# Weights of a hybrid decoder step split by transfers instead of by two engines

## The chip, the cores and the metric

The kernel runs on one core of one Trainium2 chip. Its time is the device time of one execution in microseconds, the median of three runs. The core has five engines with a queue of instructions each: TensorE (PE, its weight loads shown as PEld), VectorE (DVE), ScalarE (ACT), GpSimd (POOL) and SyncE (SP). Each runs its own queue in order; a waiting instruction holds up everything behind it on that queue. Transfers between memory (DRAM) and the core's buffers are issued from one of these queues and carried out by 16 DMA engines that all queues share.

## What is computed

One inference step of a two-layer decoder, for a prompt of 512 tokens and for 8 sequences of 8 new tokens, with the same weights; here all 576 tokens (NT) go through the dense products together. Cut to what matters:

```python
# layer A: gated linear attention (GLA), 4 heads
q, k, v, r, glow = split(rmsnorm(h, g_norm_a) @ w_in_a)        # 2048 x 6160
logg = log_sigmoid(glow @ w_gate_up + b_gate) / 16
o, S = gla_chunked(q, k, v, logg, s0)
h = h + (rmsnorm(o, g_onorm_a) * silu(r)) @ w_out_a            # 2048 x 2048
# shared keys and values, layer B: attention over a window of 128 with sinks, 32 heads
k, v = split(rmsnorm(h, g_norm_kv) @ w_kv)                     # 2048 x 512
q, z = split(rmsnorm(h, g_norm_b) @ w_in_b)                    # 2048 x 4096
h = h + (sink_attention(q, k, v) * silu(z)) @ w_out_b          # 2048 x 2048
y = rmsnorm(h, g_final)
```

Everything is float32. TensorE multiplies a rounded 32-bit format here (`float32r`), so each operand is split: its high part is the value rounded to that format, its low part is the rest. A product is taken as high x high, high part of the weights x low part of the input, and low part of the weights x high part of the input.

## The kernel before

The weights lie in DRAM as blocks of 128 output columns, each 128 partitions x 2048 numbers (16 k-tiles of 128 x 128). There are 48 blocks in `wA`, 16 in `wOA`, 4 in `wKV`, 32 in `wB` and 16 in `wOB`. `dense` makes the product of one block with all tokens. It loads the block in two halves of 8 k-tiles (512 KB each) with `load_w` (L171 to L174), a transfer issued from SP into one of three `raw` buffers. Each half is split in two quarters by `split_w` (L167 to L169): ScalarE casts a quarter of `raw` to the high part `wh`, VectorE subtracts that from `raw` into the low part `wl`; four buffers of a quarter each exist of both. Then `dense_mm` (L176 to L182) issues for every k-tile six products of 128 x 128 weights with 288 tokens: `wh` with the input's high and low part, `wl` with the input's high part, each for two halves of the tokens. They are summed in PSUM (`pd`), and a function `evac` takes the sum over.

The input's parts are the 16 tiles `X[k]`, split once per stage by ScalarE and VectorE (L96 and L97, L101 and L102).

The stages follow one another: the first two blocks and the low-rank gate while the input comes in; the 46 other blocks of `wA`, with the gated linear attention of the four heads running beside them as background chains (`gla_fronts`, `gla_backs`, `gla_samples`); the output projection `out_a` (16 blocks, with POOL adding up squares at L119 and SP storing `dh1`); four blocks for keys and values; the 32 blocks of `wB` with attention (`unit`, `unit_sample`) beside them; and the last projection, 13 blocks through `dense` and 3 that are loaded and split ahead into tiles `w` of their own and computed by halves of the tokens.

Nobody writes the order of the instructions out by hand. The program text interleaves the chains, and then a scheduler in the tile framework lays out each engine's queue from a model of how long things take and of when buffers come free. In attention, POOL's queue holds small copies into the score tiles `s` (L848 and L910; three such tiles exist).

Of the kernel before, what the change touches and what calls it, by code (L numbers as in the profile page):

```python
# [28 lines left out]
def f32(ap):  # L29
    return ap.bitcast(F32)  # L30
# [7 lines left out]
def kernel(ctx: ExitStack, tc: tile.TileContext, A, O):  # L38
# [82 lines left out]
    def make_rstd(src, n, out, b, lo=0, hi=NT):  # L121
        """out[:, t] = (sum over partitions of src[:, t] / n + eps) ** -0.5, on every partition,
        exp(-ln / 2) refined by a step of Newton's; in steps, with the banks of b"""
# [17 lines left out]
    def rstd_soon(srcs, n, b, lo, hi):  # L141
        """the same for the sum of srcs, left in the first bank of b; by columns, for few tokens"""
# [22 lines left out]
    WB = 4  # L165
# [5 lines left out]
    def load_w(wdram, blk, hf):  # L171
        raw = wp.tile([128, 8, 128], F32, tag="raw", name=nm("raw"), bufs=3)
        dma(raw, wdram[blk, :, hf * 1024:(hf + 1) * 1024].rearrange("p (k n) -> p k n", n=128))
        return raw  # L174
# [9 lines left out]
    def dense(wdram, blk, evac):  # L184
        p = pd.tile([128, 2, 512], F32, tag="d", name=nm("pd"))
        raws = [load_w(wdram, blk, hf) for hf in range(2)]
        for qt in range(4):
            wh = wp.tile([128, 4, 128], F32R, tag="wh", name=nm("wh"), bufs=WB)
            wl = wp.tile([128, 4, 128], F32R, tag="wl", name=nm("wl"), bufs=WB)
            split_w(raws[qt // 2][:, (qt % 2) * 4:(qt % 2) * 4 + 4, :], wh, wl)  # L190
            for kk in range(4):
                dense_mm(p, qt * 4 + kk, wh[:, kk, :], wl[:, kk, :], (0, 1))
                if kk % 2 == 1:
                    yield
        evac(p[:, :, :HT])
# [3 lines left out]
    def run(fg):  # L199
        """trace fg, with the steps of the background chains between its own"""  # L200
# [24 lines left out]
    with tc.tile_pool(name="gp", bufs=1) as gp:  # L225
        # ================= layer A ========================================
# [37 lines left out]
        # low-rank gate: the columns [wh | wl] three times, so that the rows of its  # L264
        # output carry what the stacked operand of the next product needs
# [9 lines left out]
        # the first two blocks and the gate's product, together as x comes in  # L275
# [12 lines left out]
        for k in range(KT):  # L288
            if k % 4 == 0:
                w0 = []  # L290
                for blk in range(2):
                    w0.append([wp.tile([128, 4, 128], F32R, tag=t, name=nm(t), bufs=WB) for t in ("wh", "wl")])
                    split_w(raws0[blk, k // 4], *w0[blk])
            split_gain(k, hpt(k), GA)
            (sso if k % 3 == 1 or k > 11 else sse).add(hpt(k))
            for blk in range(2):
                dense_mm(held[blk], k, w0[blk][0][:, k % 4, :], w0[blk][1][:, k % 4, :], (0, 1))
# [74 lines left out]
        def chunk_front(h, c, p, r):  # L372
            """scores (transposed, into scT), scaled q and k of a chunk, or of the samples (whose
            keys come twice); p is the chunk's PSUM bank"""
# [104 lines left out]
            # the pairs with their diagonal, and k by token  # L479
# [89 lines left out]
        def gla_samples():  # L569
            for h in range(NH):  # L570
# [13 lines left out]
                # for each half of the sequences: every product of a high or low part of k  # L584
                # with a high or low part of v has its rows
# [592 lines left out]
```

## Time and profile before

| | |
|---|---|
| median of 3 runs | 1793.08 us (1791.33 to 1793.31) |
| profiled execution, first to last instruction | 1791.2 us |
| PE busy | 1767.2 us (99%) |
| DVE busy | 1117.0 us (62%) |
| ACT busy | 780.5 us (44%) |
| POOL busy | 110.1 us (6%) |
| moved by the DMA engines | 231.02 MB, 129 GB/s in the mean |
| mean granted TensorE clock | 0.996 |

The profiled execution's own time is that span; the page gives no other for it. An engine's busy share does not say what bounds it. Matmuls overlap in the record, so a busy PE is judged by the pace of its instructions and by what it waited for. In the rows below a line such as `L168 ACT CAST wh<-raw 128x512 fp32r<-128x512 f32 x452 | 279.4, 618 | 589.8 <-PE pd L180 577.5` reads: the instructions of code line 168 on ScalarE, writing wh from raw, 452 of them, 279.4 us in all and 618 ns each; before them the engine stood idle for 589.8 us, 577.5 of which ended when TensorE was done with something of line 180.

### The profile page before, as it was taken

Reading aid. Unit: us, or ns where it says so; the run is one execution under the profiler, and the core shown is the slowest. Engines: PE = TensorE matmul, PEld = TensorE weight load, DVE = VectorE, ACT = ScalarE, POOL = GpSimd, SP = SyncE. Lnnn points to the kernel's source line nnn. Section 1 sums busy time; section 2 is a strip of 40 time slices with the busy share of each in tenths; the row PEclk is TensorE's granted clock in tenths of the full one; section 3 lists DMA queues with packets and bytes.
Section 4 is the critical chain, followed back from the end, with each engine's and each line's share of the span. In section 5 each row is a group of like instructions: output and inputs, shape, how many; then the busy total and the mean of one; then the engine's idle time right before and its main releaser. Section 6 shows DMA issues by size and latency. Waiting matters only on the chain.

```text
span 1791.2 us, 33731 instructions
## 1 busy us (share of the span) xinstructions
PE 1767.2 (99%) x13152; PEld 1748.8 (98%) x13152; DVE 1117.0 (62%) x2539; ACT 780.5 (44%) x1632; POOL 110.1 (6%) x190
## 2 busy tenths in 40 slices
PE   8999999999999999999999999999999999999997
PEld 7999999999999999999999999999999999999996
DVE  8576776786776886544222566888888873442234
ACT  7533334334444344343222555667666652332231
POOL 3000001001001001000010100100000000001110
PEclk9999999999999999999999999999999999999998
DMA  8245643564564343223333444343332222223323
GB/s 301 89 160 176 195 156 117 176 197 136 161 194 158 119 154 135 96 77 124 128 131 127 134 134 110 88 126 101 105 99 88 85 94 82 83 98 108 104 106 106
DMA packets 118767, 231.02 MB, mean 129 GB/s; under 512 B 22064, under 2 KB 49584, under 8 KB 118576
## 3 DMA queue, kind: packets, MB, share of 16 engines
q1 hardware_dynamic: 118608, 228.88, 39.4%
q8 instruction: 103, 1.69, 0.4%
q14 instruction: 56, 0.46, 0.1%
HBM read 174.57 MB, written 43.65 MB: 122 GB/s over the span
## 4 chain that ended last, share of the span: by engine, by line
PE 94%; issue 2%; DMA 2%; DVE 1%; ACT 0%; POOL 0%; POOLq 0%; DVEq 0%; SPq 0%; ACTq 0%
PE pd L180 79%; PE pb L463 2%; PE pb L863 1%; PE pb L550 1%; DMA hp<-in_xT_dram 1%; PE pb L846 1%; PE pb L639 1%; PE pb L638 1%; PE pb L636 1%; PE pb L845 1%; PE pb L551 1%; PE pb L873 1%; PE pb L874 1%; PE pb L481 1%; PE pb L558 0%
## 5 line engine op out<-in xcount | busy, mean ns | idle before, releaser
L180 PE MATMUL pd<-x,wh 128*128 128x288 f32 x7232 | 1305.0, 298 | 9.8 <-ACT x L96 6.7
L180 PEld LDWEIGHTS pd<-x,wh 128*128 128x128 f32 x7232 | 1080.2, 189 | 17.4 <-ACT x L96 6.7
L180 PE MATMUL pd<-x,wl 128*128 128x288 f32 x3616 | 791.8, 298 | 0.7 <-DVE wl L169 0.6
L180 PEld LDWEIGHTS pd<-x,wl 128*128 128x128 f32 x3616 | 587.6, 189 | 4.1 <-DVE wl L169 1.4
L168 ACT CAST wh<-raw 128x512 fp32r<-128x512 f32 x452 | 279.4, 618 | 589.8 <-PE pd L180 577.5
L169 DVE TENSOR_TENSOR wl<-raw,wh 128x512 fp32r<-128x512 f32 x452 | 316.4, 701 | 337.7 <-ACT wh L168 336.1
L119 POOL TENSOR_TENSOR acc<-acc,st 128x576 f32<-128x576 f32 x46 | 70.3, 1528 | 323.2 <-ACT st L114 322.4
L855 ACT ACTIVATE s<-s,tiny 128x257 f32<-128x257 f32 (+1 forms) x128 | 60.9, 478 | 19.8 <-DVE tiny L853 19.6
L618 ACT CAST sh<-Si 128x512 fp32r<-128x512 f32 x64 | 39.7, 620 | 66.9 <-PE pb L638 43.9
L114 ACT ACTIVATE st<-hp 128x576 f32<-128x576 f32 (+2 forms) x66 | 43.3, 664 | 56.8 <-DVE hp L1045 28.6
L117 POOL COPY acc<-st 128x576 f32<-128x576 f32 x7 | 5.5, 779 | 907.6 <-ACT st L114 907.6
L640 DVE SCALAR_TENSOR_TENSOR Si<-Si,dl,pb 128x512 f32<-128x512 f32 x64 | 47.6, 744 | 12.2 <-PE pb L636 11.4
L619 DVE TENSOR_TENSOR sl<-Si,sh 128x512 fp32r<-128x512 f32 x64 | 44.4, 693 | 13.6 <-PE pb L639 5.5
L850 DVE SCALAR_TENSOR_TENSOR s<-distp,pb 128x256 f32<-128x256 f32 (+1 forms) x128 | 43.9, 383 | 11.2 <-PE pb L846 10.6
L867 ACT CAST pTh<-pb 128x256 fp32r<-128x256 f32 (+1 forms) x64 | 34.0, 532 | 29.7 <-PE pb L863 28.2
L868 DVE TENSOR_TENSOR pTl<-pb,pTh 128x256 fp32r<-128x256 f32 (+1 forms) x64 | 39.6, 620 | 8.4 <-ACT pTh L867 7.7
L878 ACT COPY hp<-pb 64x128 f32<-64x128 f32 x128 | 33.3, 260 | 25.5 <-PE pb L874 14.7
L438 ACT ACTIVATE E<-E 128x2304 f32<-128x2304 f32 (+1 forms) x20 | 37.5, 1875 | 15.3 <-DVE E L435 15.3
L97 DVE SCALAR_TENSOR_TENSOR x<-hp,c_vecs,x 128x576 fp32r<-128x576 f32 x48 | 42.1, 913 | 2.0 <-ACT x L96 2.0
L879 DVE TENSOR_TENSOR hp<-hp,pb 64x128 f32<-64x128 f32 x128 | 36.2, 283 | 9.2 <-ACT hp L878 6.6
L863 PE MATMUL pb<-c_ident,s 128*128 128x128 f32 x224 | 40.6, 273 | 0.0
L853 DVE TENSOR_REDUCE tiny<-s 128x2 f32<-128x258 f32 (+1 forms) x64 | 39.3, 616 | 1.7
(234 smaller groups left out, 1803.2 us busy)
## 6 DMA issues: line engine op xcount, KB each, us to landing
raw<-in_wA_dram SPq DMA_DIRECT2D x92, 512.0 KB
raw<-in_wB_dram SPq DMA_DIRECT2D x64, 512.0 KB
Si<-in_state_dram SPq DMA_DIRECT2D x64, 256.0 KB
out_gla_sample_dram<-Si SPq DMA_DIRECT2D x64, 256.0 KB
raw<-in_wOA_dram SPq DMA_DIRECT2D x32, 512.0 KB
raw<-in_wOB_dram SPq DMA_DIRECT2D x32, 512.0 KB
dqkb<-st SPq DMA_DIRECT2D x24, 288.0 KB
hp<-in_xT_dram SPq DMA_DIRECT2D x16, 288.0 KB
```

The source lines that it names most:

```text
L97: vec.scalar_tensor_tensor(t[:, 1, :], src, g, f32(t[:, 0, :]), ALU.mult, ALU.subtract)
L114: act(sq[:, lo:hi], src, AF.Square)
L119: self.eng.tensor_tensor(self.acc[:, lo:hi], self.acc[:, lo:hi], sq[:, lo:hi], ALU.add)
L168: nc.scalar.copy(wh, raw)
L169: vec.tensor_tensor(wl, raw, f32(wh), ALU.subtract)
L180: mm(p[:, a, :HT], w, x[:, part, a * HT:(a + 1) * HT], start=(k == 0 and w is wh and part == 0), stop=(k == KT - 1 and w is wl))
L618: nc.scalar.copy(sh, Si)
L619: vec.tensor_tensor(sl, Si, f32(sh), ALU.subtract)
L640: vec.scalar_tensor_tensor(Si, Si, dl[:, f * 16 + i:f * 16 + i + 1], p, ALU.mult, ALU.add)
L850: vec.scalar_tensor_tensor(s[:, e, off:256], distp[:, off:256], slope(2 * m + e), p[:, e * 256 + off:(e + 1) * 256], ALU.mult, ALU.subtract)
L855: act(s[:, e, off:257], s[:, e, off:257], AF.Exp, scale=-1.0, bias=tiny[:, e:e + 1], accum_out=tiny[:, 2 + e:3 + e])
L863: nc.tensor.transpose(out=p[:, (hf * 2 + e) * 128:(hf * 2 + e + 1) * 128], in_=s[:, e, off + hf * 128:off + (hf + 1) * 128], identity=ident)
```

## The change

`dense` no longer loads `raw` and no longer splits on ScalarE and VectorE. A new function `parts` makes both parts of a half block of 8 k-tiles: a transfer issued from POOL writes `wh` from DRAM and casts to the rounded format on the way; ScalarE writes the negative of `wh` into `wl`; a second transfer from POOL reads the same weights from DRAM again and adds them to what stands in `wl`. The buffers are now of a half block each, three of `wh` and four of `wl`, which together take the room that `raw`, `wh` and `wl` took. The first two blocks are still loaded to `raw` and split as before, into halves of the new buffers; so are the last three, whose `raw` tiles lie in another pool now.

```diff
-    WB = 4
+    WB = (("wh", 3), ("wl", 4))
 
     def split_w(raw, wh, wl):
         nc.scalar.copy(wh, raw)
         vec.tensor_tensor(wl, raw, f32(wh), ALU.subtract)
 
-    def load_w(wdram, blk, hf):
-        raw = wp.tile([128, 8, 128], F32, tag="raw", name=nm("raw"), bufs=3)
-        dma(raw, wdram[blk, :, hf * 1024:(hf + 1) * 1024].rearrange("p (k n) -> p k n", n=128))
-        return raw
+    def parts(src):
+        wh, wl = (wp.tile([128, 8, 128], F32R, tag=t, name=nm(t), bufs=b) for t, b in WB)
+        nc.gpsimd.dma_start(wh, src)
+        act(wl, f32(wh), AF.Copy, scale=-1.0)
+        nc.gpsimd.dma_start(wl, src, accum_op=ALU.add)
+        return wh, wl
...
     def dense(wdram, blk, evac):
         p = pd.tile([128, 2, 512], F32, tag="d", name=nm("pd"))
-        raws = [load_w(wdram, blk, hf) for hf in range(2)]
-        for qt in range(4):
-            wh = wp.tile([128, 4, 128], F32R, tag="wh", name=nm("wh"), bufs=WB)
-            wl = wp.tile([128, 4, 128], F32R, tag="wl", name=nm("wl"), bufs=WB)
-            split_w(raws[qt // 2][:, (qt % 2) * 4:(qt % 2) * 4 + 4, :], wh, wl)
-            for kk in range(4):
-                dense_mm(p, qt * 4 + kk, wh[:, kk, :], wl[:, kk, :], (0, 1))
+        for hf in range(2):
+            wh, wl = parts(wdram[blk, :, hf * 1024:(hf + 1) * 1024].rearrange("p (k n) -> p k n", n=128))
+            for kk in range(8):
+                dense_mm(p, hf * 8 + kk, wh[:, kk, :], wl[:, kk, :], (0, 1))
                 if kk % 2 == 1:
                     yield
...
         for k in range(KT):
             if k % 4 == 0:
-                w0 = []
+                if k % 8 == 0:
+                    w0 = [[wp.tile([128, 8, 128], F32R, tag=t, name=nm(t), bufs=b) for t, b in WB] for _ in range(2)]
                 for blk in range(2):
-                    w0.append([wp.tile([128, 4, 128], F32R, tag=t, name=nm(t), bufs=WB) for t in ("wh", "wl")])
-                    split_w(raws0[blk, k // 4], *w0[blk])
+                    split_w(raws0[blk, k // 4], *(t[:, k % 8:k % 8 + 4] for t in w0[blk]))
...
             for hf in range(2):
-                raw = load_w(A["wOB"], j, hf)
+                raw = tp.tile([128, 8, 128], F32, tag="raw", name=nm("raw"), bufs=3)
+                dma(raw, A["wOB"][j, :, hf * 1024:(hf + 1) * 1024].rearrange("p (k n) -> p k n", n=128))
```

The queues as the scheduler lays them out now, at the places of interest (the number behind a name tells buffers apart; `wh` and `wl` with neighbouring numbers are one half block). POOL's queue in the output projection `out_a` holds only the sum of squares before:

```order
L117 COPY acc_9287<-st_9285 128x576
L119 TENSOR_TENSOR acc_9287<-acc_9287,st_9410 128x576
L119 TENSOR_TENSOR acc_9287<-acc_9287,st_9534 128x576
L119 TENSOR_TENSOR acc_9287<-acc_9287,st_9658 128x576
L119 TENSOR_TENSOR acc_9287<-acc_9287,st_9783 128x576
```

and after:

```order
L177 DMA wl_9730<-in_wOA_dram 128x1024
L175 DMA wh_9782<-in_wOA_dram 128x1024
L177 DMA wl_9783<-in_wOA_dram 128x1024
L175 DMA wh_9843<-in_wOA_dram 128x1024
L119 TENSOR_TENSOR acc_8809<-acc_8809,st_9722 128x576
L177 DMA wl_9844<-in_wOA_dram 128x1024
L175 DMA wh_9896<-in_wOA_dram 128x1024
```

Transfers of `wh` and `wl` alternate there; each `wl` waits for ScalarE's negation of the `wh` ahead of it, and each `wh` for TensorE to have left its buffer. ScalarE's queue at the same place before, where `st` are the squares:

```order
L168 CAST wh_9505<-raw_9419 128x512
L114 ACTIVATE st_9410<-hp_1274_9283 128x576
L168 CAST wh_9545<-raw_9541 128x512
L168 CAST wh_9573<-raw_9541 128x512
L168 CAST wh_9601<-raw_9543 128x512
```

and after:

```order
L114 ACTIVATE st_8807<-hp_984_8805 128x576
L176 ACTIVATE wl_8930<-wh_8929 128x1024
L176 ACTIVATE wl_8983<-wh_8982 128x1024
L114 ACTIVATE st_8922<-hp_984_8805 128x576
L176 ACTIVATE wl_9044<-wh_9043 128x1024
```

Four casts of a quarter for each block have become two negations of a half, between the same squares. In attention POOL's queue holds copies into `s` and `qs` before:

```order
L848 COPY s_13696<-sinkp 128x2
L834 CAST qs_13207<-stE_13869 128x8x8
L834 CAST qs_13207<-stO_13870 128x8x8
L848 COPY s_13756<-sinkp 128x2
L848 COPY s_13798<-sinkp 128x2
```

and after:

```order
L175 DMA wh_13132<-in_wB_dram 128x1024
L849 COPY s_12709<-sinkp 128x2
L177 DMA wl_13133<-in_wB_dram 128x1024
L835 CAST qs_12483<-stE_12867 128x8x8
L835 CAST qs_12483<-stO_12868 128x8x8
L175 DMA wh_13251<-in_wB_dram 128x1024
L849 COPY s_12758<-sinkp 128x2
L849 COPY s_12800<-sinkp 128x2
L177 DMA wl_13252<-in_wB_dram 128x1024
```

The transfers of the weights have come between the copies, so that copies now stand between a half's `wh` and its `wl`.

## Rows read from the trace of the kernel before

**Rows 1.** The page: span, and busy us (share of the span) xinstructions
```profile
span 1791.2 us, 33731 instructions
PE 1767.2 (99%) x13152; PEld 1748.8 (98%) x13152; DVE 1117.0 (62%) x2539; ACT 780.5 (44%) x1632; POOL 110.1 (6%) x190
```
**Rows 2.** The timeline of TensorE in a dense stretch: start us, us, instructions merged
```profile
900.60 0.69 PE L180 MATMUL pd<-x,wh 128*128 128x288 f32 x4
901.13 0.43 PE L180 MATMUL pd<-x,wl 128*128 128x288 f32 x2
901.40 0.70 PE L180 MATMUL pd<-x,wh 128*128 128x288 f32 x4
```
**Rows 3.** Windows: busy us of each engine by stage, granted clock, DMA share, GB/s
```profile
100.00:700.00 600.00, 600.00 (x4321) 585.18 (x4321) 442.78 (x1157) 240.50 (x427) 17.46 (x12) 1.00 0.51 162
700.00:1040.00 340.00, 340.00 (x2541) 338.97 (x2541) 141.51 (x202) 114.51 (x181) 29.52 (x24) 1.00 0.34 114
1040.00:1480.00 440.00, 439.49 (x3437) 439.29 (x3436) 346.20 (x889) 280.74 (x794) 29.95 (x126) 1.00 0.35 104
1480.00:1740.00 260.00, 260.00 (x1951) 260.00 (x1950) 97.16 (x142) 78.10 (x126) 16.83 (x13) 1.00 0.29 98
```
**Rows 4.** The same windows for line 180 alone: dense matmuls, then their weight loads
```profile
100.00:700.00 600.00, 484.51 (x3283) 457.83 (x3283) 1.00 0.51 162
700.00:1040.00 340.00, 337.26 (x2521) 336.27 (x2521) 1.00 0.34 114
1040.00:1480.00 440.00, 381.92 (x2577) 349.50 (x2576) 1.00 0.35 104
1480.00:1740.00 260.00, 257.80 (x1934) 257.56 (x1932) 1.00 0.29 98
```
**Rows 5.** Groups by line: count, busy us, mean ns, idle us before them and releasers
```profile
L169 DVE TENSOR_TENSOR wl<-raw,wh 128x512 fp32r<-128x512 f32 x452 | 316.4, 701 | 337.7 <-ACT wh L168 336.1 <-PE pb L863 0.3 <-issue 0.2
L168 ACT CAST wh<-raw 128x512 fp32r<-128x512 f32 x452 | 279.4, 618 | 589.8 <-PE pd L180 577.5 <-issue 5.6 <-DMA raw<-in_wA_dram 3.0
L119 POOL TENSOR_TENSOR acc<-acc,st 128x576 f32<-128x576 f32 x46 | 70.3, 1528 | 323.2 <-ACT st L114 322.4
...
L848 POOL COPY s<-sinkp 128x2 f32<-128x2 f32 x64 | 15.8, 248 | 255.5 <-PE pb L863 111.7 <-DMA out_k_win_sample_dram<-kw 31.0 <-PE pb L926 16.0
...
L346 ACT ACTIVATE hp<-hp 128x1152 f32<-128x1152 f32 x4 | 4.7, 1172 | 0.1
```
**Rows 6.** The chain that ended last, at the start: start us, us, what
```profile
39.21 1.20 DVE wl L169 x2
...
41.87 1.28 DVE wl L169 x2
```
**Rows 7.** Timeline of SP's queue near the end: loads of 512 KB issued
```profile
1713.62 0.33 SPq L173 DMA_DIRECT2D raw<-in_wOB_dram  x1
...
1720.31 0.93 SPq L173 DMA_DIRECT2D raw<-in_wOB_dram  x2
...
1725.89 0.33 SPq L173 DMA_DIRECT2D raw<-in_wOB_dram  x1
```
**Rows 8.** Timeline of ScalarE there: casts that waited for these loads
```profile
1718.33 1.15 ACT L168 CAST w<-raw 128x512 fp32r<-128x512 f32 x2 [2.49 <-DMA raw<-in_wOB_dram]
...
1723.92 2.41 ACT L168 CAST w<-raw 128x512 fp32r<-128x512 f32 x4 [1.68 <-DMA raw<-in_wOB_dram]
...
1730.04 1.14 ACT L168 CAST w<-raw 128x512 fp32r<-128x512 f32 x2 [1.45 <-DMA raw<-in_wOB_dram]
```
**Rows 9.** The first 50 us: their window, and a link of the chain
```profile
0.00:50.00 50.00, 39.47 (x261) 37.78 (x262) 41.80 (x55) 34.02 (x54) 14.62 (x14) 1.00 0.77 279
5.02 6.20 DMA hp<-in_xT_dram
```
**Rows 10.** Timeline of TensorE after its last wait at the start
```profile
49.91 0.77 PE L180 MATMUL pd<-x,wh 128*128 128x288 f32 x4 [2.31 <-DVE st L250]
...
50.88 1.16 PE L180 MATMUL pd<-x,wh 128*128 128x288 f32 x4
```

More of the change, by code (lines that the diff above doesn't have):

```diff
@@ L296 @@
             for blk in range(2):
-                dense_mm(held[blk], k, w0[blk][0][:, k % 4, :], w0[blk][1][:, k % 4, :], (0, 1))
+                dense_mm(held[blk], k, w0[blk][0][:, k % 8, :], w0[blk][1][:, k % 8, :], (0, 1))
             if 3 <= k < 3 + KG:
```

## The prediction

> **What bounds the kernel now.** I read the page first: the span is 1791.2 us and TensorE is busy for 99% of it [rows 1]. Matmuls overlap, so that share alone proves little; the pace does. In a stretch of nothing but dense products the four high-part matmuls of one k-tile start at 900.60 and those of the next at 901.40 [rows 2]: 0.80 us for six matmuls, so 6.40 us for a half block of eight k-tiles, and no idle time is noted before them. Next come the stages [rows 3]: TensorE's busy time fills 100 to 700 us (the GLA stage), 700 to 1040 (the last gate blocks and the output projection, dense alone), 1040 to 1480 (attention) and 1480 to 1740 (dense again), all at a granted clock of 1.00. Then how many dense matmuls each holds [rows 4]; 48 make a half block, so these are 68.4, 52.5, 53.7 and 40.3 halves at 600/68.4 = 8.77, 340/52.5 = 6.48, 8.19 and 6.45 us each. The split of the weights runs beside this and is early: ScalarE's 452 casts were mostly waiting for TensorE to give a buffer back (577.5 of 589.8 us), and VectorE's subtraction waited for that cast [rows 5]. So VectorE (62%) and ScalarE (44%) are covers, not bounds [rows 1]. Faster engines there give nothing back in these 1640 us; what can be lost is the supply of weights.
>
> **The change, part by part.** *Removed.* 444 of the 452 casts of 0.618 us and subtractions of 0.701 us go (8 remain, for the first two blocks): 274 us of ScalarE, 311 us of VectorE [rows 5]. Both hide under TensorE, so the worth is nothing, but for the start: there two pieces of subtractions for the next block, 1.20 and 1.28 us, stand in the chain that leads to the first rstd [rows 6]. That is up to 2.5 us, if nothing else takes their place.
>
> *Added on ScalarE.* 222 negations of 128x1024. A 128x512 cast takes 0.618 us and a 128x1152 activation 1.172 [rows 5], 0.87 ns for each further column, so 1.06 us each, 235 us in all: about what was removed.
>
> *Added on POOL and the DMA engines.* 444 transfers of 512 KB take the place of 222 from SP. POOL's row now reads wh, wl, wh, wl, and wl waits for ScalarE's negation, which waits for wh to land. The next wh stands behind that wait. So this is a loop which must turn once in each half: POOL writes wh's descriptors, wh lands, ScalarE negates, POOL writes wl's descriptors. The trace of before has no transfer from POOL, so each term is bounded by neighbours.
> - Landing. Three lone 512 KB loads went from issue to the cast that waited for them in 1713.62 to 1718.33 = 4.71, 1720.31 to 1723.92 = 3.61 and 1725.89 to 1730.04 = 4.15 us, 0.33 us of it on the issuing queue [rows 7, 8]. I take 4.15 - 0.33 = 3.82 (3.28 to 4.38).
> - POOL's time for one transfer. Not below SP's 0.33 us; as an upper end the longest frequent thing that POOL does, 1.528 us [rows 5]. Nothing tells where between; I take the middle, 0.93, twice.
> - Negation 1.06 us, and two hand-overs of about 0.05.
>
> The loop is 0.93 + 3.82 + 0.05 + 1.06 + 0.05 + 0.93 = 6.84 us (5.10 to 8.60). In the two dense stages a half has 6.40 to 6.48 us, so the loop is late by about 0.4 us each time: 92.8 x 0.4 = 37 us. The three wh and four wl buffers hide delay of a single half, not a rate; they do hide wl's own landing, since 6.84 + 4.15 = 11 us is less than the two halves (12.9 us) that TensorE still has when a buffer comes free.
>
> In the GLA stage a half has 8.77 us, but transfers share the engines. Share 0.51 at 162 GB/s means 318 GB/s when busy, so 1.65 us of all 16 engines for 512 KB [rows 3]. Per half that is 0.51 x 8.77 = 4.47 us before, and 1.65 more (or 3.30, if the transfer that adds has to move both operands) after: 70 to 89% busy. In the first 50 us, with 77% busy, a wait for one landing lasted 6.20 us [rows 9], 2.05 more than 4.15. With that, and 0.3 us behind ScalarE's other work (40% busy, operations of about half a microsecond), the loop is 9.19 us: 68.4 x 0.42 = 29 us. In attention the engines reach 55 to 75% and ScalarE is busy 64% [rows 3]; half a microsecond for each gives 7.9, and some of POOL's little copies ahead of wl bring it to 8.3 against 8.19: 53.7 x 0.1 = 5 us. SP's queue only loses work: its 222 loads into raw and their waits go, so other loads and stores leave earlier. The squares' additions on POOL (46 of 1.53 us) stand between wh and wl, under wh's landing, and cost nothing unless a square is late.
>
> The sum on the execution's span: 1791.2 + 37 + 29 + 5 = 1862, less half of the 2.5 at the start; the runs' median lies 1.9 us above that span, so **1863 us**. Loop ends of 5.10 and 8.60 make this 1793 (nothing shows) and 1791 + 92.8 x 2.15 + 68.4 x 2.2 + 53.7 x 1.9 = about 2240.
>
> The Trainium skill's page "DMA: Bandwidth & Descriptors", section "Anatomy of one DMA", puts a transfer from GpSimd at about 2.0 us plus bytes over 436 GB/s, an estimate of 3.2 us for this size, below all three landings above. By it the loop would be some 5.3 us in the dense stages, under 6.40: the first rival. The rows disagree by 0.4 to 1.5 us, for transfers of another queue.
>
> **The rivals.**
> *Nothing shows.* If POOL's descriptors take about 0.5 us and landings 3.6, the loop is 5.7 us, and TensorE hides it in every stage. For it: one of three landings was that short, and wh is asked for two halves ahead. Against: two were not, and POOL's work is slow elsewhere. It gives 1793, or 1790.6 with the start's 2.5 us. It decides where the loop is under 6.4 us. This is the case that is not slower.
> *The DMA engines become the bound.* If transfers that cast or add run at half the plain rate, a half needs 3.3 us for wh and 3.3 to 6.6 for wl beside the other traffic (0.55 us in the dense stages, 2.8 in GLA, 1.2 in attention): 7.2 to 10.5, 9.4 to 12.7 and 7.8 to 11.1 us. Sum: +107 to +800 us, 1900 to 2590, its middle 2240. [...] For it: no row shows the rate of such a transfer. Against: at plain rates the dense stages come to 0.34 x 6.48 + 1.65 or 3.30 of 6.48 us, 59 to 85%.
> The skill's page "Collectives: The Full Stack", section "The bandwidth ceiling", says that an adding transfer is halved by its two source reads and not by the addition. By that alone the engines stay at 85 to 89%, no bound; it speaks for the forecast's side.
> *Queues lock into each other in attention.* POOL's 64 copies into `s` waited 255.5 us, 4 us each, for TensorE and others [rows 5], which cost nothing. Now wl's transfer stands behind them, and ScalarE's negation ahead of softmax work. If attention runs late against this order, each half loses 2 to 4 us: 53.7 x 3 = 160, with the dense stages' 37 some 1990. Against: the order was laid out with these waits in it, and before, nothing in attention held TensorE.
> *Faster.* Only the start can give: 1788 would need twice the 2.5 us.
> That the change does not do what it says can be excluded: the new order shows the 444 transfers on POOL.
>
> **How the numbers follow.** Forecast 0.41, nothing shows 0.28 (with its 2.5 us gain it stays within 0.2%, about what a measurement of this kernel can tell from no change, 3.6 us), DMA engines 0.16, locked queues 0.11, faster 0.04. Faster 0.04, same 0.28, slower 0.68. The forecast's own range is 1800 to 1960. Since no change at all holds 0.28, the range begins at 1789; upward it takes in the locked queues and the lower part of the DMA case and stops at 2100, leaving out about 0.13 above.
>
> **What would show it.** Right: in 700 to 1040 TensorE waits for wl (or the transfer into it) by some tenths of a microsecond in nearly every half, halves are 6.8 us apart, POOL goes from wh to wl to wh without rest, and ScalarE waits for wh's landing instead of for TensorE. The first rival: POOL waits for TensorE before each wh. The second: DMA share near 1.0. The third: dense stages unchanged, attention longer. Wrong altogether if POOL's transfers land within 3 us, or take over 8 each.

## The result

The kernel became slower: 2191.74 us (2176.8 to 2194.1) against 1793.19 (1791.33 to 1794.21) for the kernel before, a ratio of 1.2203 with a 95% interval of 1.2166 to 1.2241. The direction was forecast, and the mechanism too (a loop through POOL's queue), but not its size: 2192 lies above the forecast's 1863 and above the range's end of 2100.

The page of the changed kernel, where columns are as in [rows 1]:

```profile
span 2190.3 us, 33182 instructions
PE 1884.4 (86%) x13152; PEld 1827.9 (83%) x13152; DVE 835.0 (38%) x2095; ACT 732.8 (33%) x1410; POOL 421.4 (19%) x634
```

Against [rows 1] the span is 399 us longer. TensorE stands idle for 2190.3 - 1884.4 = 306 us instead of 24, which is 282 of them; the other 117 are in its busy time, 1884.4 instead of 1767.2 for the same 13152 matmuls. The windows of the old stages, which answer to [rows 3], show where most of the second part comes from, the granted clock, 0.95 instead of 1.00:

```profile
100.00:700.00 600.00, 533.75 (x3623) 513.17 (x3622) 286.33 (x823) 184.30 (x292) 98.35 (x129) 0.95 0.74 188
700.00:1040.00 340.00, 289.88 (x1994) 279.56 (x1993) 114.83 (x257) 90.88 (x130) 61.57 (x80) 0.95 0.63 151
```

Over the whole span the mean clock is 0.953 instead of 0.996; as an estimate from these means, the lower clock makes at most (1 - 0.953) x 2190.3 - (1 - 0.996) x 1791.2 = 96 of the 117 us, and the rest wasn't traced. The share of the DMA engines (next to last) rose from 0.51 to 0.74 and from 0.34 to 0.63, far from 1. The loss lies in every stage. These are the issues of the weights' loads, L173 of the kernel before and then L175 of the changed one: shortest, median and longest ns, first and last start in us.

```profile
L173 SPq DMA_DIRECT2D raw<-in_wA_dram x92: 327/333/1311, 20.6 to 777.2; - x92
L173 SPq DMA_DIRECT2D raw<-in_wB_dram x64: 327/333/584, 1050.2 to 1540.6; - x64
L173 SPq DMA_DIRECT2D raw<-in_wOA_dram x32: 327/328/411, 783.8 to 982.0; - x32
```

```profile
L175 POOL DMA_DIRECT2D wh<-in_wA_dram x92: 537/672/909, 25.0 to 940.5; - x92
L175 POOL DMA_DIRECT2D wh<-in_wB_dram x64: 547/622/892, 1304.4 to 1889.4; - x64
L175 POOL DMA_DIRECT2D wh<-in_wOA_dram x32: 722/853/881, 949.3 to 1220.8; - x32
```

The dense stage `wOA` is the plainest: 31 steps between 32 halves took (982.0 - 783.8)/31 = 6.39 us each and now take (1220.8 - 949.3)/31 = 8.76. By the last load of each stage the delay grows to 163 us by the end of `wA`, 239 by the end of `wOA`, 349 by the end of `wB`, and 399 at the end.

What each half waits for is in the timeline of that stage (start us, us, engine and line, idle time before and its releaser). POOL's rows:

```profile
1105.73 0.86 POOL L177 DMA_DIRECT2D wl<-in_wOA_dram  x1 [6.78 <-ACT wl L176]
1106.30 0.85 POOL L175 DMA_DIRECT2D wh<-in_wOA_dram  x1
1106.88 1.72 POOL L119 TENSOR_TENSOR acc<-acc,st 128x576 f32<-128x576 f32 x1
1114.84 0.88 POOL L177 DMA_DIRECT2D wl<-in_wOA_dram  x1 [6.24 <-ACT wl L176]
1115.43 0.84 POOL L175 DMA_DIRECT2D wh<-in_wOA_dram  x1
1123.88 0.87 POOL L177 DMA_DIRECT2D wl<-in_wOA_dram  x1 [7.60 <-ACT wl L176]
```

and ScalarE's negation between them:

```profile
1113.48 1.06 ACT L176 ACTIVATE wl<-wh 128x1024 fp32r<-128x1024 f32 x1 [7.48 <-issue]
1122.52 1.06 ACT L176 ACTIVATE wl<-wh 128x1024 fp32r<-128x1024 f32 x1 [7.98 <-DMA wh<-in_wOA_dram]
```

The second negation waits for the landing of `wh`; for the first the profile names no releaser ("issue"), but it starts as late behind its transfer. From issue to landing the two transfers take here (KB each, median us):

```profile
wh<-in_wOA_dram POOLq DMA_DIRECT2D x32, 512.0 KB, 6.9
wl<-in_wOA_dram POOLq DMA_DIRECT2D x32, 512.0 KB, 6.2
```

The loop stands here step by step. `wl` is issued at 1105.73, the next `wh` 0.57 us later; ScalarE starts the negation 7.18 us after that, and the next `wl` goes out 1.36 us after the negation's start (1.06 of it the negation): 9.11 us. The next turn, 1114.84 to 1123.88, takes 9.04. In the sums of the waits POOL waits for the negation (all stages), the negation for the landing (here in `wA`) and TensorE for the adding transfer (here in `wOA`); each row gives the engine, its tile and line, what it waited for, then us in all, times, longest:

```profile
POOL wl L177 <- ACT wl L176: 1254.5, 186, 9.8
ACT wl L176 <- DMA wh<-in_wA_dram: 396.8, 78, 10.6
PE pd L184 <- DMA wl<-in_wOA_dram: 54.8, 31, 2.9
```

In `wOA`, a stage of 32 halves, TensorE waited for the adding transfer 31 times, 1.8 us each in the mean. What the clock did behind one of the longer waits:

```profile
1112.22 0.53 PE L184 MATMUL pd<-x,wl 128*128 128x288 f32 x2 [2.50 <-DMA wl<-in_wOA_dram]
1112.59 0.69 PE L184 MATMUL pd<-x,wh 128*128 128x288 f32 x4
...
1113.54 1.16 PE L184 MATMUL pd<-x,wh 128*128 128x288 f32 x4
...
1114.98 1.16 PE L184 MATMUL pd<-x,wh 128*128 128x288 f32 x4
```

After 2.50 us of idle time the engine first runs at its pace, and then from 1113.2 to 1116.4 four matmuls take 1.16 us instead of 0.69: a granted clock of 0.50 there, the lower of its two levels, 1.2 GHz. So such a wait costs more than its own length. Not every wait did: of the 31, ten (2.0 to 2.9 us) were followed by such a stretch, while five of 2.3 to 2.7 us and all the shorter ones were not.

### The profile page after: what moved, and what is told of

Same layout as the page of the kernel before. It is cut to its first block, busy times and chain, and to the rows that moved or that the text cites. A ratio compares the mean times of both kernels' runs of the same rounds, so it can differ in the third digit from the quotient of the medians.

```text
span 2190.3 us, 33182 instructions
## 1 busy us (share of the span) xinstructions
PE 1884.4 (86%) x13152; PEld 1827.9 (83%) x13152; DVE 835.0 (38%) x2095; ACT 732.8 (33%) x1410; POOL 421.4 (19%) x634
## 4 chain that ended last, share of the span: by engine, by line
issue 35%; PE 11%; POOL 8%; DMA 6%; DVE 1%; ACT 1%; SPq 0%; POOLq 0%; DVEq 0%; ACTq 0%
PE pd L184 8%; DMA wh<-in_wB_dram 4%; POOL wl L177 3%; POOL wh L175 3%; POOL acc L119 2%; PE pb L864 1%; ACT wl L176 1%; DMA stO<-ql 1%; DMA wl<-in_wB_dram 0%; PE pb L846 0%; PE pb L874 0%; DMA cv<-in_cacheV_dram 0%; PE pb L847 0%; PE pb L875 0%; DMA wh<-in_wKV_dram 0%
## 5 line engine op out<-in xcount | busy, mean ns | idle before, releaser
L184 PE MATMUL pd<-x,wh 128*128 128x288 f32 x7232 | 1349.6, 306 | 14.9 <-ACT x L96 6.6
L184 PEld LDWEIGHTS pd<-x,wh 128*128 128x128 f32 x7232 | 1126.7, 197 | 23.4 <-ACT x L96 6.5
L184 PE MATMUL pd<-x,wl 128*128 128x288 f32 x3616 | 828.0, 309 | 189.9 <-DMA wl<-in_wOA_dram 54.8
L176 ACT ACTIVATE wl<-wh 128x1024 fp32r<-128x1024 f32 x222 | 235.1, 1059 | 1115.0 <-DMA wh<-in_wA_dram 396.8
L177 POOL DMA_DIRECT2D wl<-in_wA_dram x92 | 80.2, 872 | 654.7 <-ACT wl L176 587.7
L177 POOL DMA_DIRECT2D wl<-in_wB_dram x64 | 56.1, 877 | 348.0 <-ACT wl L176 243.5
L175 POOL DMA_DIRECT2D wh<-in_wA_dram x92 | 64.9, 705 | 110.8 <-PE pd L184 94.4
L177 POOL DMA_DIRECT2D wl<-in_wOA_dram x32 | 27.9, 872 | 214.8 <-ACT wl L176 214.8
L175 POOL DMA_DIRECT2D wh<-in_wB_dram x64 | 44.8, 699 | 41.6 <-PE pd L184 36.5
L464 PE MATMUL pb<-E 128*128 128x192 f32 (+1 forms) x208 | 43.2, 343 | 7.2 <-DVE scT L474 3.7
```

The source lines that it names most:

```text
L175: nc.gpsimd.dma_start(wh, src)
L176: act(wl, f32(wh), AF.Copy, scale=-1.0)
L177: nc.gpsimd.dma_start(wl, src, accum_op=ALU.add)
L184: mm(p[:, a, :HT], w, x[:, part, a * HT:(a + 1) * HT], start=(k == 0 and w is wh and part == 0), stop=(k == KT - 1 and w is wl))
L464: mm(p[:, o:o + N], keys(li)[:, f * 128:(f + 1) * 128], queries(li)[:, f, :], start=(f == 0), stop=(f == 1))
```

## The experiments

Two theories stood first. Theory A is the loop just read: `wl`'s issue, the next `wh` landing behind it on the same queue, the negation, `wl`'s issue. Theory B is the second rival: the DMA engines' rate with twice the weights' bytes. Theories C, D, E and F came with the later runs and are named in their expectations. Times are medians, or single runs where it says so; the kernel before took 1794 us beside each of them.

**The transfers by themselves.** All of the kernel's work is replaced by runs of twelve 512 KB transfers, each waiting for the one before: plain from SP (L57), plain from POOL (L59), casting from POOL (L61), adding from POOL (L63); then twelve turns of the kernel's own loop, in which the negation is followed by an adding transfer into `wl` and a casting one into `wh`, both from POOL (L67 to L69); and twelve turns in which the second of these is a plain one from SP, into tiles `vl` and `vh` (L73 to L75).

```diff
+    for i in range(N):
+        nc.gpsimd.dma_start(one, src(3 * N + i), accum_op=ALU.add)
...
+    for i in range(N):
+        act(wl, f32(wh), AF.Copy, scale=-1.0)
+        nc.gpsimd.dma_start(wl, src(4 * N + i), accum_op=ALU.add)
+        nc.gpsimd.dma_start(wh, src(5 * N + i))
```

> All of the model is left out; 512 KB transfers one after another, each waiting for the last to land: twelve plain from SP, twelve plain from POOL, twelve casting from POOL, twelve adding from POOL; then twelve turns of negation, adding transfer and casting transfer back to back from POOL; then the same with the second one plain from SP. If a casting transfer is slow by itself: 6 us or more alone. If it is slow because it stands behind the adding one in the same queue: 4 to 4.8 us alone, about 7 in the pair, and 4 to 5 when it comes from SP instead. My terms of 4.15 us for a landing (SP) and 4.75 (POOL) hold if plain ones from SP land in 3.6 to 4.2 and from POOL in 4 to 5.

From issue to landing, a median of 3.3 us plain from SP (3.0 to 3.6), 3.6 plain from POOL (3.3 to 4.0), 3.6 casting (3.3 to 3.8) and 5.4 adding (5.0 to 5.6). In the loop the casting transfer, which now stands right behind an adding one on the same queue, takes 6.2 (6.0 to 7.1), as the page of this run has it (transfers, KB each, median us from issue to landing; the first line is the plain ones from SP, `wl` and `wh` are the loop, `vl` and `vh` the turns with SP):

```profile
one<-in_wA_dram SPq DMA_DIRECT2D x12, 512.0 KB, 3.3
wl<-in_wA_dram POOLq DMA_DIRECT2D x12, 512.0 KB, 5.5
wh<-in_wA_dram POOLq DMA_DIRECT2D x12, 512.0 KB, 6.2
vh<-in_wA_dram SPq DMA_DIRECT2D x12, 512.0 KB, 4.2
vl<-in_wA_dram POOLq DMA_DIRECT2D x12, 512.0 KB, 7.3
```

The lone casting and adding transfers (L61, then L63), shortest, median and longest:

```profile
DMA to landing us min/median/max: 3.3/3.6/3.8
DMA to landing us min/median/max: 5.0/5.4/5.6
```

Two turns of the loop:

```profile
263.28 1.06 ACT L67 ACTIVATE wl<-wh 128x1024 fp32r<-128x1024 f32 x1 [7.08 <-DMA wh<-in_wA_dram]
264.72 0.87 POOL L68 DMA_DIRECT2D wl<-in_wA_dram  x1 [6.72 <-ACT wl L67]
265.26 0.89 POOL L69 DMA_DIRECT2D wh<-in_wA_dram  x1
271.31 1.06 ACT L67 ACTIVATE wl<-wh 128x1024 fp32r<-128x1024 f32 x1 [6.97 <-DMA wh<-in_wA_dram]
```

One turn is 271.31 - 263.28 = 8.03 us, and from 205.5 to 298.1 eleven turns took 8.42 each, with not one other transfer under way. So this loop can't keep up with 6.4 us a half even in an empty machine. It isn't the casting that is dear: alone it costs what a plain load costs. The terms of 4.15 and 4.75 us for lone landings from SP and POOL don't hold, they were too high. In the turns with SP the plain transfer goes out ahead of the adding one (306.9 and 307.3 us in the first turn, 404.1 and 404.4 in the last); it takes 4.2 us, and the adding one, now second, 7.3 instead of 5.4. So the one that goes out second pays across two queues as well, and the loss isn't a matter of one shared queue alone. The Trainium skill's page "DMA: Bandwidth & Descriptors", section "Anatomy of one DMA", whose fixed time plus bytes for a transfer from GpSimd gave an estimate of 3.2 us, comes out 0.4 us below the plain and the casting transfers from POOL (3.6 each); it doesn't hold for the adding one (5.4) or for what goes out behind it (6.2).

**No adding.** The second transfer casts instead of adding, so that `wl` holds the weights; everything else, the order and the loop too, is left.

```diff
-        nc.gpsimd.dma_start(wl, src, accum_op=ALU.add)
+        nc.gpsimd.dma_start(wl, src)
```

> The second transfer casts like the first and does not add (the low part comes out as the high part, so it is wrong); negation, order and dependences stay. Theory A with a fixed landing: 2130 to 2200 us, since the loop and wh's landing stay. Theory A where wh lands late because it stands in the queue behind wl's adding transfer (which moves two operands): wh lands about 1.5 us earlier, the loop is 7.5 us, dense halves 7.5, time 1930 to 2010. Theory B: time falls by the share that the addition has in the DMA engines' time, 1900 to 2050, with the DMA share above 0.6 still.

1932.65 us (one run; the kernel before 1794.3 on the same chip). In `wOA` the casting `wh` lands 5.0 us after its issue, against 6.9, and the loop shrinks from 8.76 us, as the issues of `wh` there show:

```profile
L175 POOL DMA_DIRECT2D wh<-in_wOA_dram x32: 537/537/554, 842.9 to 1066.4; - x32
```

(1066.4 - 842.9)/31 = 7.21 us a half. So 259 of the 399 us hang on the adding, but the loop without it is still longer than 6.4 us, and 138 us of loss stay. The number lies in the range of theory A with a late landing and in that of theory B, so this run by itself doesn't part them.

**The loop cut at the negation.** The negation reads a constant instead of `wh` and so doesn't wait for its landing. All transfers are left; `wl` then holds the weights.

```diff
-        act(wl, f32(wh), AF.Copy, scale=-1.0)
+        act(wl, ones.rearrange("p (a n) -> p a n", a=1).broadcast_to([128, 8, 128]), AF.Copy, scale=0.0)
```

> The negation reads a constant instead of wh (times zero), so that the second transfer no longer depends on the first: wl comes out as the weights themselves, so the low part of the weights is wrong, every transfer, negation and product is still there. Theory A (the loop on POOL's queue: wh must land and be negated before wl's transfer and the next wh can be issued; 9.0 us per half in the dense stages of the changed kernel): the loop is gone, dense halves return to 6.4 to 6.6 us, time 1795 to 1840 us. Theory B (the transfers themselves are the bound: cast and add are slow on the DMA engines and share one queue): a half still needs about 8 to 9 us in the dense stages, time above 2050. Between 1850 and 2050 both have a part.

1860.78 us (one run), far under theory B's 2050, but 21 us above theory A's 1840, so by its own expectation both may have a part. 331 of the 399 us come back although every byte and every adding transfer is still there. From 845 to 1040 us, most of `wOA`, TensorE is busy all the time at full clock, with the DMA engines at 0.89 (columns as in [rows 3]), busier than the 0.63 of the slow kernel:

```profile
845.00:1040.00 195.00, 195.00 (x1465) 195.00 (x1464) 25.72 (x36) 51.81 (x63) 63.97 (x76) 1.00 0.89 203
```

By its waits, POOL and ScalarE now stand for TensorE to give buffers back, as where supply is ample:

```profile
POOL wh L175 <- PE pd L184: 861.4, 193, 14.5
ACT wl L176 <- PE pd L184: 511.6, 139, 6.5
```

**The loop cut by order.** The same computation as the changed kernel, but the next half's casting transfer (`high` issues that of a half, unless it is out already) goes out ahead of this half's adding one, so that it no longer stands behind the wait for the negation; four high and three low buffers instead of three and four.

```diff
-    WB = (("wh", 3), ("wl", 4))
+    WB = (("wh", 4), ("wl", 3))
...
+        high(i)
+        high(i + 1)
...
+        with tc.issue_after(highs[-1][1].ins):
+            nc.gpsimd.dma_start(wl, half(i), accum_op=ALU.add)
```

> Nothing is left out. The next half's wh transfer is issued ahead of this half's wl transfer (four wh buffers and three wl instead of three and four), so wh lands while POOL still has the adding transfer to issue. Theory A (the loop): per half POOL no longer waits for a landing that it has just issued, dense halves 6.4 to 6.6 us, time 1793 to 1840, and TensorE's clock back above 0.99. Theory B (the DMA engines or their queue): as slow as the changed kernel, 2050 to 2200 us.

1863.64 us (1857.07 to 1881.57), ratio 1.0374 (1.0354 to 1.0393): what the constant gave, within the spread, and like it above theory A's 1840 (the clock, in the mean 0.984, missed the 0.99 expected too). This version changes two things, order and buffers, and the next two take them apart.

**The order, with the changed kernel's buffers** (three and four):

```diff
-    WB = (("wh", 4), ("wl", 3))
+    WB = (("wh", 3), ("wl", 4))
```

> The casting transfer issued one half ahead of the adding one, but with the changed kernel's own buffers, three high and four low (the kernel at 1864 us has four high and three low). Theory E (a second loop: a high tile is freed, filled in 5.2 us, negated in 1.06, and its low tile lands 8 us after its issue, some 15 us for two halves of 6.4): 7.4 to 7.9 us a half and 2000 to 2060 us. Theory F (order alone cuts the loop; what made the kernel with deeper state loads slow, 2047 us, was these loads): 1850 to 1885 us.

2059.9 us (2050.4 to 2069.7), ratio 1.1481 (1.1440 to 1.1522). The order alone gives back 132 us; now a second loop binds, that of the high buffer. By the waits POOL stands for TensorE before each `wh`, yet TensorE stands for `wl`:

```profile
POOL wh L179 <- PE pd L201: 1267.1, 203, 20.5
PE pd L201 <- DMA wl<-in_wA_dram: 34.7, 33, 2.3
```

The issues of `wh` in `wOA`, for their step:

```profile
L179 POOL DMA_DIRECT2D wh<-in_wOA_dram x32: 560/562/612, 910.8 to 1158.7; - x32
```

A freed high tile is filled in 5.3 us, negated in 1.06, and its low tile lands 8.0 us after its issue, together with some 0.5 us of hand-overs 14.9 us, for which three buffers leave two halves of 6.4. That is 7.4 us a half at least; the measured step is (1158.7 - 910.8)/31 = 8.00, above the 7.4 to 7.9 expected, and the other 0.6 us weren't traced.

**The buffers, with the changed kernel's text:**

```diff
-    WB = (("wh", 3), ("wl", 4))
+    WB = (("wh", 4), ("wl", 3))
```

> The changed kernel's order with four high and three low buffers. Theory A (the loop through POOL's queue, 9.0 us a half, does not hang on buffers): 2150 to 2200 us. Theory E alone (the high tile's release sets the half, POOL's order does not matter): 1870 to 1960 us.

1867.57 us (1866.1 to 1877.7), ratio 1.0425 (1.0393 to 1.0457). The number is next to theory E's 1870, but the kernel didn't hold the order still, as its expectation had assumed. The scheduler sets the order from a model in which buffers come free, and with a fourth high buffer it issues each `wh` one half earlier by itself. POOL's queue in `out_a`, first of the changed kernel and then of this one (the `wl` numbered one above a `wh` is of the same half):

```
L177 DMA wl_1013_9211<-in_wOA_dram 128x1024
L175 DMA wh_1018_9272<-in_wOA_dram 128x1024
L177 DMA wl_1019_9273<-in_wOA_dram 128x1024

L175 DMA wh_1018_9272<-in_wOA_dram 128x1024
L177 DMA wl_1013_9211<-in_wOA_dram 128x1024
L175 DMA wh_1020_9325<-in_wOA_dram 128x1024
L177 DMA wl_1019_9273<-in_wOA_dram 128x1024
```

So it is the kernel with the order ahead once more (1864 and 1868), and not a test of buffers at the old order; that combination wasn't run. What the pair settles: 132 us come from the order at three high buffers, and 192 to 196 more from four high and three low buffers once the order is right.

**Only the casting transfer.** `wl` is again VectorE's subtraction, from a plain load on SP's queue; three buffers of `wh`, two each of `wl` and `raw`. The bytes are those of the changed kernel.

```diff
-        act(wl, f32(wh), AF.Copy, scale=-1.0)
-        nc.gpsimd.dma_start(wl, src, accum_op=ALU.add)
+        for q in (slice(0, 4), slice(4, 8)):
+            vec.tensor_tensor(wl[:, q], raw[:, q], f32(wh[:, q]), ALU.subtract)
```

> Only the casting transfer is kept: the high part still comes from POOL's casting transfer, the low part is again VectorE's raw minus high from a plain load on SP's queue, so the bytes moved are those of the changed kernel (345 MB) but no adding transfer stands in front of the casting one and no negation hangs on it. Theory A (the loop wl issue -> wh transfer landing behind it -> negation -> wl issue sets the half): the loop is gone and a casting transfer lands in 3.6 us alone, so 1793 to 1830 us. Theory B (the bytes of a second full transfer of the weights bound the kernel through the DMA engines): at least 1950 us, as the bytes are unchanged.

1831.87 us (1825.3 to 1834.3), ratio 1.0204 (1.0184 to 1.0225): 2 us above theory A's range and far under theory B's 1950. Twice the weights' bytes don't bound the kernel.

**Only the adding transfer.** ScalarE rounds the high part from a plain load and negates it; two buffers of each of `raw` and `wh`, three of `wl`.

```diff
-        nc.gpsimd.dma_start(wh, src)
+        for q in (slice(0, 4), slice(4, 8)):
+            nc.scalar.copy(wh[:, q], raw[:, q])
```

> Only the adding transfer is kept: ScalarE rounds the high part from a plain load on SP's queue, negates it, and POOL's queue carries nothing of the weights but the adding transfers. Theory A: each adding transfer lands 5.4 to 7.5 us after its issue but nothing waits behind it on its queue and the next negation does not hang on it, so the loop is gone; what stays is the adding transfers' hold on the DMA engines, as in the two kernels with the loop cut: 1800 to 1870 us. Theory B (bytes): at least 1950 us.

2174.88 us (2169.4 to 2186.3), ratio 1.2142 (1.2099 to 1.2184): neither theory's reason, but the number of theory B. The waits of its trace, below, show why it proves nothing yet. ScalarE's rounding waits for TensorE to leave a high tile, and with only two of these each low part has to be made within one half:

```profile
ACT wh L178 <- PE pd L187: 659.7, 148, 11.1
PE pd L187 <- DMA wl<-in_wA_dram: 74.5, 42, 5.0
```

So it was run again with three high buffers and one `raw`:

```diff
-    WB = (("wh", 2), ("wl", 3))
+    WB = (("wh", 3), ("wl", 3))
...
-        raw = wp.tile([128, 8, 128], F32, tag="raw", name=nm("raw"), bufs=2)
+        raw = wp.tile([128, 8, 128], F32, tag="raw", name=nm("raw"), bufs=1)
```

> Only the adding transfer kept (high part by ScalarE from a plain load), with three high buffers and one raw instead of two and two. Theory E (in the kernel with two high buffers, 2175 us, a high tile was freed, rounded in 1.14, negated in 1.06, and its low tile landed 7 us later: 9.6 us for one half of 6.4): with two halves for these 9.6 us the low parts come in time, 1800 to 1880 us, what is above 1793 from the adding transfers' hold on the DMA engines. Theory B (222 adding transfers cost this by themselves): at least 2100 us.

1891.89 us (1881.7 to 1901.4), ratio 1.0543 (1.0498 to 1.0589), 12 us above the expected range. With one more high buffer (and one `raw` fewer) 283 us are gone. Bytes and adding transfers cost some 100 us here at most; the rest of that kernel's loss was a high buffer too few.

**What the adding still costs without the loop.** The kernel with the constant, its second transfer casting instead of adding.

```diff
-        nc.gpsimd.dma_start(wl, src, accum_op=ALU.add)
+        nc.gpsimd.dma_start(wl, src)
```

> As the kernel whose negation reads a constant (1861 us), and the second transfer casts instead of adding; so the low part is the weights rounded, not the remainder. Theory C (what stayed of the loss, 67 us, is that adding transfers keep the DMA engines busy, so that the state loads of the GLA stage land late): the time falls to 1793 to 1820 us and ScalarE's waits for the state tiles (76 us) fall under 20 us. Theory D (what stayed comes from the other order of work on ScalarE and VectorE): 1850 to 1865 us.

1816.47 us (1812.9 to 1828.8), ratio 1.0136 (1.0099 to 1.0173), as theory C forecast. This closes the square (1860.8 and 1932.7 are single runs):

| | loop through the queue | loop cut by the constant |
|---|---|---|
| second transfer adds | 2191.7 | 1860.8 |
| second transfer casts | 1932.7 | 1816.5 |

The adding costs 259 us inside the loop and 44 outside; the loop costs 331 with it and 116 without. The two add up to more than their sum because the adding transfer is a part of the loop: `wh` lands behind it.

What the adding costs outside the loop lies in the GLA stage. The last load of `wA` goes out at 777.2 in the kernel before, at 838.4 with constant and adding, at 796.3 with constant and casting; behind it the three need about the same time, 1014, 1021 and 1015 us to the end. And ScalarE waits there for the state tiles, 75.9 us with the adding (first) and 17.3 without (second), 0.5 before. In the form of the waits above:

```profile
ACT sh L619 <- DMA Si<-in_state_dram: 75.9, 22, 8.4
```

```profile
ACT sh L619 <- DMA Si<-in_state_dram: 17.3, 5, 4.9
```

**State tiles loaded earlier.** The kernel with the order ahead, its state tiles loaded four steps ahead instead of two, into six buffers instead of four, paid for with the fourth high buffer.

```diff
-    WB = (("wh", 4), ("wl", 3))
+    WB = (("wh", 3), ("wl", 3))
...
-                Ss = [load(0), load(1)]
+                Ss = [load(n) for n in range(4)]
```

> The kernel with the casting transfer issued one half ahead (1864 us), with the GLA stage's state tiles loaded four steps ahead instead of two (six buffers instead of four; paid for by three buffers of the high part instead of four). Theory C (state loads land late behind busy DMA engines): ScalarE's waits for the state tiles (77 us) fall under 30 us and the time to 1800 to 1840 us. Theory D (other order of the engines' work): 1855 to 1870 us.

2047.32 us (2041.1 to 2052.5), ratio 1.1409 (1.1385 to 1.1434). The waits for the state tiles fall to 5.7 us, but the fourth high buffer is gone too, and with three the kernel takes 2060 us, as seen above; this run says nothing on C or D. The same on the kernel with the constant, which keeps its three high buffers and pays with a low one:

```diff
-    WB = (("wh", 3), ("wl", 4))
+    WB = (("wh", 3), ("wl", 3))
...
-                Ss = [load(0), load(1)]
+                Ss = [load(n) for n in range(4)]
```

> The kernel whose negation reads a constant (1861 us; its low part is the weights instead of the remainder), with the GLA stage's state tiles loaded four steps ahead into six buffers instead of two steps into four, and three low buffers instead of four to pay for them. There ScalarE waits 76 us for state tiles and the wA stage ends 61 us late. Theory C (state loads land late behind adding transfers): these waits fall under 15 us and the time to 1800 to 1835 us. Theory D (other order of the engines' work, state loads only beside it): 1850 to 1870 us.

1851.62 us (1849.7 to 1861.1), ratio 1.0330 (1.0303 to 1.0357), against one run of 1860.78. The waits for state tiles fall to 12.8 us and almost nothing comes of it: theory C's time is missed, and theory D's is met, while the kernel with constant and casting had met C's and missed D's; so neither holds as it was put. The stage now waits for other small transfers, most of all the heads' own tensors on their way through DRAM. The largest such wait of ScalarE in this kernel:

```profile
ACT dl L441 <- DMA kb<-dqkb: 53.9, 10, 15.1
```

Before, that wait was 10.9 us in seven times. So the late state tiles were one place where lateness showed, not its cause. That adding holds up the stage's small transfers in general would fit the 44 us of the square, but which of them set the time wasn't separated, nor were the 22 us that stay with two casting transfers and the 38 with only the casting one.

## Why the prediction was wrong

**Removed work, right as far as seen.** ScalarE's 274 us and VectorE's 311, both under TensorE, were priced at nothing. No run takes them away alone, but none that does came out faster: with constant and casting VectorE is busy for 838.5 us instead of 1117.0, and the time is 1816.

**The mechanism, right.** The loop is there as the forecast named it: POOL goes from `wl` to `wh` without a rest, ScalarE waits for `wh`'s landing, POOL for the negation, TensorE for the transfer into `wl`. Cutting it gives 331 of the 399 us back.

**The loop's length, wrong, and this is the step that failed.** The terms against their measurements in `wOA`:

| term | predicted, us | measured, us |
|---|---|---|
| POOL, from `wl`'s issue to `wh`'s | 0.93 | 0.57 |
| `wh`, from its issue to the negation's start | 0.93 + 3.82 + 0.05 = 4.80 | 7.18 |
| negation | 1.06 | 1.06 |
| from its end to `wl`'s issue | 0.05 | 0.30 |
| a turn | 6.84 | 9.11 |

The landing was the mis-sized term: 3.82 us in bounds of 3.28 to 4.38, with POOL's time 4.75 from the issue, taken from three plain loads [rows 7, 8] that it called lone. As the price of a lone transfer that was too much: a lone casting one took 3.6 us from its issue, and a plain one from SP 3.3 where 4.15 were taken. But in this order `wh` is not alone. It goes out 0.57 us behind an adding transfer of the same size on the same queue and lands after 6.2 us in an empty machine and 6.9 in the kernel. So the direction came out right by luck: with the measured lone landing the sum is 0.57 + 3.6 + 1.06 + 0.30 = 5.5 us, hidden under 6.4, and what made the kernel slower is that `wh` goes out behind the other transfer of the weights, which the sum doesn't have. The prediction wrote that `wl`'s own landing is hidden under the buffers, which was half of the truth: it is hidden from TensorE and stands in the loop all the same, in front of `wh`. One of the three loads had a second right behind it, from the same queue (the two at 1720.31 in [rows 7]), but both were plain and no wait shows when the second landed; so the bounds should have run from one landing to two, 4 to 8 us; then the loop's upper end would have been 8.60 - 4.38 + 8.0 = 12.2 us, far on the other side of what came. Even the forecast's own loop end of 8.60 gave 2240, above the 2192 measured; the range stopped at 2100 all the same.

The same error made the stages too cheap: 2.4 us a half in `wOA` instead of 0.4 or 0.5, and a delay of 163 us by the end of `wA` where 29 were given for the GLA stage and some 5 for the twelve halves behind it.

**The clock, left out of the sum.** In [rows 10] four matmuls take 1.16 us behind a wait of 2.31, but the sum has no term for it. Here the 117 us of extra busy time, up to 96 of them the clock by the estimate above, are over a quarter of the loss. Where long waits are rare the clock stays higher: 0.984 in the kernel with the loop cut and in the one without adding, 0.953 in the changed one.

**The buffers as cover, wrong.** The prediction let three high buffers hide everything but the rate, with a `wl` landing of 4.15 us in a sum of 11 us against 12.9. With the queue's loop cut and the same buffers, `wl` took 8.0 us and the sum 14.9: a second bound of 8.0 us a half under the first, 2060 us. It didn't set this kernel's time, but it caught the repair that changed the order alone.

**The rivals.** *Nothing shows* needed a loop under 6.4 us; the shortest steps measured with this loop in place, with nothing adding, were 7.21 us in `wOA` and (1860.7 - 1684.6)/25 = 7.04 in `wOB`. *The DMA engines become the bound* named a price near the truth for the wrong reason: the engines are at 0.63 to 0.74, and kernels with the same bytes run at 1832 and 1892, one with every adding transfer at 1861. The adding transfers do hold the engines longer, 32.2% of 16 engines over 2168.1 us for 222 of them, or 3.14 us each, where 222 casting ones took 22.7% of 1832.5, 1.87 us each: 1.68 times. The queue that POOL feeds, in the kernel with only adding and then in that with only casting (packets, MB, share):

```profile
q0 software_dynamic: 31968, 116.41, 32.2%
q0 software_dynamic: 31968, 116.41, 22.7%
```

The Trainium skill's page "Collectives: The Full Stack", section "The bandwidth ceiling", whose two source reads would make it about twice, overstates that but points the right way, and the prediction was wrong to take from it that no harm follows: the harm came as latency in a loop, and not as a rate. *Locked queues in attention* isn't what took the time: of POOL's waits in front of `wl` for something other than the negation, by name, the largest is

```profile
POOL wl L177 <- ACT hp L879: 58.4, 11, 7.5
```

and the longest of these eleven shows the loop again, for the negation ends 0.29 us before `wl` goes out, and the copy of L879 merely follows it:

```profile
1532.37 1.06 ACT L176 ACTIVATE wl<-wh 128x1024 fp32r<-128x1024 f32 x1 [2.70 <-DMA wh<-in_wB_dram]
1533.72 0.87 POOL L177 DMA_DIRECT2D wl<-in_wB_dram  x1 [7.52 <-ACT hp L879]
```

`wB` grows by some 95 us, to (1889.4 - 1304.4)/63 = 9.29 us a half; in the kernel with the constant, whose weights still share POOL's queue with the copies, a half takes (1619.4 - 1117.9)/63 = 7.96 us, near the 7.78 before. *Faster* had no ground.

## What to carry to other kernels

Before splitting one load into two dependent transfers, write down what stands in a row on the issuing queue, and close the loop: if a transfer's issue waits for a result of the one before, each landing in that row is paid once per turn, and a transfer right behind another lands later than alone (behind an adding one 6.9 us in this kernel, 3.6 alone). Buffers and a lookahead have to cover that whole row, and order and buffers have to be changed together, since the order alone gave back only a part. With TensorE 99% busy, as here, freeing other engines had nothing to give, and the second reading of the weights brought only its costs.

## What the runs showed of the hardware

- Casting on the way costs a lone transfer nothing: 3.6 us for 512 KB from POOL, as a plain one. Adding costs 1.8 us more alone (5.4), and 1.68 times the DMA engines' time.
- A casting transfer right behind an adding one on its queue lands after 6.2 us instead of 3.6. In the reverse order the adding one pays: `wl` 7.8 and `wh` 5.2 us in `wOA` (the kernel with four high buffers), against `wl` 6.2 and `wh` 6.9 in the changed kernel. It pays across queues too: 7.3 us from POOL, 0.3 us behind a plain transfer from SP, which took 4.2.
- POOL shows 0.86 us for issuing an adding transfer at 1105.73, yet issues the next after 0.57.
- After a wait of 2.50 us TensorE ran at full pace for about one microsecond and then 3.2 us at half the clock, with the clock back at 1.00 under the work that followed. After a wait of 2.66 us that ended at 1042.51 the clock stayed at 1.00. Windows behind the two, in the columns of [rows 3]:

```profile
1113.20:1116.40 3.20, 3.20 (x15) 3.20 (x14) 0.00 (x0) 1.06 (x1) 1.44 (x2) 0.50 0.00 0
1117.00:1121.00 4.00, 3.39 (x26) 3.16 (x24) 0.76 (x1) 0.00 (x0) 0.00 (x0) 1.00 0.94 209
1042.50:1049.00 6.50, 6.49 (x48) 6.40 (x48) 0.34 (x1) 1.06 (x1) 1.45 (x2) 1.00 0.32 46
```
